# First slabs split and multiplied by single k, and the mixed activations moved behind the split weights, in a one-core decoder layer

## The chip, the cores and the metric

One NeuronCore of a Trainium2 chip runs the whole layer in one launch. The metric is the device time of that launch in microseconds (us); lower is better. Engines are named as the profile names them: PE is TensorE (matmuls), PEld its weight loads, DVE is VectorE, ACT is ScalarE, POOL is GpSimd, SP is SyncE, which here only issues DMAs.

## What is computed

One decoder layer on x of shape (1, 256, 2048), all in float32. Cut to what matters here:

```python
hn = rmsnorm(x, norm_mix_g)
p = hn @ w_in + b_in                        # 2048 x 7176: conv a and g, q, k, v, o, gates
u = silu(group_norm(causal_dwconv(p_a * sigmoid(p_g))))
hm = group_norm(mlstm(q, k, v, gates)) * sigmoid(p_o)
x = x + concat([u, hm]) @ w_out             # 2048 x 2048
hf = rmsnorm(x, norm_ffn_g)
up = hf @ w_up                              # 2048 x 11264
x = x + (silu(causal_dwconv(up[:, :5632])) * up[:, 5632:]) @ w_down   # 5632 x 2048
return rmsnorm(x, norm_final_g)
```

## The kernel before, in words

**Split matmuls.** Each float32 operand is written as a sum of a rounded part `hi` (type fp32r) and a remainder `lo`. A product is then three matmuls: hi by hi, hi by the other's low part, lo by hi. The weights come from memory in *slabs* of two k blocks of 128 rows by 512 columns (512 KB, 128 x 1024 in SBUF). `load(i)` (line 173) brings slab i into one of five `raw` buffers, by DMAs on SP's queue; `split` (190) and `split_part` (207) make `hi` by a cast on ACT (line 214; for one half of slab 0 by a copy on DVE, line 212) and `lo` by a subtraction on DVE or POOL (line 215). There are four buffers for each of `hi` and `lo`.

**The order of work** is written out by hand: each engine runs its instructions in the order in which the Python code issues them, and waits for others by semaphores. The loop over slabs (line 993) issues for slab i the load of slab i + 5, the splits of slabs ahead, the matmuls of slab i, and then what other work has been put on the list for this slab (`tasks`, `after`, `bg`). Splits run up to three slabs ahead.

**The start.** Slabs 0 to 7 are the first column group of the convolution's projection, `ws_group` (line 225): there the weights are the stationary operand (128 x 128 blocks, four column blocks `ct` for each k) and 256 columns of x, transposed, the moving one (tile `xp`, `xT["h"]` and `xT["l"]`). x itself is transposed beside them. `prep_x(c)` (line 924) does this for the two k blocks of slab c: four transposes on PE into a PSUM bank (line 928), the high part on ACT, scaled by the norm's gain (931), the low part on DVE (934). It is called from inside the matmuls of the slab before, by `mid_hook` (lines 235 and 1007). The DMAs on SP are, in order: the gain's rows, slab 0, x for slab 1, slab 1, x for slab 2, slab 2 and so on; x for slab 0 comes on ACT's queue. Slabs 0 and 1 are loaded in two DMAs of one k each (line 183), later slabs of this group in two DMAs of one column half each (185).

Ahead of slab 0, PE is given warm-up transposes of the identity matrix, `warm_pe` (949): six, then the transposes of the gain, five more, x's first block (k = 0 of slab 0), ten more. Slab 0 is split in halves, one for each k; x's second block and the second half come after the twelve matmuls of the first k, the transposes of x for slab 1 after six more.

The matmuls of a `ws` slab run k by k and, inside, ct by ct: three products on the same column block (lines 241 to 243) and then the next block.

**Where tiles lie.** Tile pools are laid one behind the other in SBUF: `cst`, then `slab` (five `raw`, four `hi`, four `lo`, 4,096 bytes per partition each), then `mid`. Within `mid`, tiles lie in the order in which they are first asked for: seven row tiles of 512 bytes, `bb` of 8,224 bytes, then `mixh` and `mixl` of 16,384 bytes each (lines 304 and 305), then the rest. When the feed-forward part begins, `mid` is closed and a pool `ffn` opens in its place (`open_ffn`), with `ah` and `al` first.

`mixh` and `mixl` are the split, concatenated outputs of the two head groups. They are the stationary operand of the output projection (w_out): `xs_slab` (line 277) with the slab's `hi` and `lo` as the moving operand of 512 columns, lines 286 to 288. The down projection runs the same lines with `ah` and `al`.

Of the kernel before, what the change touches and what calls it, by code (L numbers as in the profile page):

```python
# [9 lines left out]
F32 = mybir.dt.float32  # L10
F32R = mybir.dt.float32r
AF = mybir.ActivationFunctionType
# [3 lines left out]
P = 128  # L16
T = 256
NT = T // P
D = 2048
NK = D // P  # L20
# [14 lines left out]
SPLIT_BUFS = 4  # L35
AHEAD = 3
SIG = 4
WARM = (6, 5, 10)


@with_exitstack
def hybrid_layer_kernel(
# [7 lines left out]
    act, dve, pool, pe = nc.scalar, nc.vector, nc.gpsimd, nc.tensor  # L50
# [7 lines left out]
    mid = inner.enter_context(tc.tile_pool(name="mid", bufs=1))  # L58
# [3 lines left out]
    def mm_bank(name):  # L62
        return ps.tile([P, 512], F32, tag="mm", name=name, bufs=4)

    def cv_bank(k, name):
        return ps.tile([P, 512], F32, tag=f"cv{k}", name=name)

    def ax_bank(name):
        return ps.tile([P, 512], F32, tag="ax", name=name, bufs=2)
# [6 lines left out]

    def v2(t):
        return t.rearrange("p (a b) -> p a b", a=2)


    ident = cst.tile([P, P], F32, tag="ident", name="ident")
# [56 lines left out]
    g_mix = cst.tile([P, NK], F32, tag="cG", name="cG")  # L138
# [5 lines left out]
    def transpose_rows(*items):  # L144
        b = ax_bank("tr")
        o = 0
        for key, dst in items:
            r, n = rows[key]
            pe.transpose(b[:, o:o + n], r[:n, :], ident[:n, :n])
            o += n  # L150
        o = 0
        for key, dst in items:
            n = rows[key][1]
            act.copy(dst, b[:, o:o + n])
            o += n
# [6 lines left out]
    slabs = []  # L162
    tasks = defaultdict(list)
    bg = deque()
    cur = [0]

    def after(delay, fn, cost=0.0):
        tasks[cur[0] + delay].append((fn, cost))

    raw_t, hi_t, lo_t = {}, {}, {}  # L170
    mid_hook = []

    def load(i):
        if i >= len(slabs):
            return
        s = slabs[i]
        t = slab.tile([P, 2 * W], F32, tag="raw", name=f"raw{i}", bufs=RAW_BUFS)
        d = t[:, :s["nk"] * s["w"]]
        if len(s["src"].shape) == 4:
            d = d.rearrange("p (k s c) -> p k s c", k=s["nk"], s=2)  # L180
            for h in range(2):
                if i < 2:
                    nc.sync.dma_start(d[:, h], s["src"][:, h])
                else:
                    nc.sync.dma_start(d[:, :, h], s["src"][:, :, h])
        else:
            nc.sync.dma_start(d.rearrange("p (k c) -> p k c", k=s["nk"]), s["src"])
        raw_t[i] = t

    def split(i):  # L190
        if i >= len(slabs):
            return
        split_part(i, 0, 1, *split_tiles(i))

    def split_tiles(i):
        s = slabs[i]
        n = s["nk"] * s["w"]
        raw = raw_t.pop(i)
        hi = slab.tile([P, 2 * W], F32R, tag="hi", name=f"hi{i}", bufs=SPLIT_BUFS)
        lo = slab.tile([P, 2 * W], F32R, tag="lo", name=f"lo{i}", bufs=SPLIT_BUFS)  # L200
        s["eng"] = pool if s["pool"] and i >= 8 and i % 2 else dve
        hi_t[i] = hi[:, :n].rearrange("p (k c) -> p k c", k=s["nk"])
        lo_t[i] = lo[:, :n].rearrange("p (k c) -> p k c", k=s["nk"])
        s["lo"] = 0.0 if s["eng"] is pool else 1.1 * n + 30
        return raw, hi, lo

    def split_part(i, h, parts, raw, hi, lo):
        s = slabs[i]
        n = s["nk"] * s["w"]
        c = slice(h * n // parts, (h + 1) * n // parts)  # L210
        if h + 1 < parts:
            dve.tensor_copy(hi[:, c], raw[:, c])
        else:
            act.copy(hi[:, c], raw[:, c])  # L214
        s["eng"].tensor_sub(lo[:, c], raw[:, c], hi[:, c].bitcast(F32))  # L215

    def w_slab(wap, kt, nk, col, w, fn, on_pool):
        if col is None:
            src = wap(kt)
        else:  # L220
            src = wap[kt * P:(kt + nk) * P, col:col + w].rearrange("(k p) c -> p k c", p=P)
        slabs.append(dict(src=src, w=w, nk=nk, mm=fn, pool=on_pool))


    def ws_group(wap, col, mov, nk, done, on_pool):
        st = {}

        def mk(kt):
            def fn(hi, lo):
                if kt == 0:  # L230
                    st["b"] = [mm_bank("ws0"), mm_bank("ws1")]
                mh, ml = mov()
                for k in range(2):
                    for ct in range(4):
                        if mid_hook and mid_hook[0][0] == (k, ct):
                            mid_hook.pop(0)[1]()
                        o = v2(st["b"][ct // 2])[:, ct % 2, :]
                        cs = slice(ct * P, (ct + 1) * P)
                        first = kt + k == 0 and ct % 2 == 0
                        last = kt + k == nk - 1  # L240
                        pe.matmul(o, hi[:, k, cs], mh[:, kt + k, :], start=first, stop=False, skip_group_check=True)  # L241
                        pe.matmul(o, hi[:, k, cs], ml[:, kt + k, :], start=False, stop=False, skip_group_check=True)  # L242
                        pe.matmul(o, lo[:, k, cs], mh[:, kt + k, :], start=False, stop=last, skip_group_check=True)  # L243
                if kt + 2 == nk:
                    done(st["b"])
            return fn

        for kt in range(0, nk, 2):
            w_slab(wap, kt, 2, col, W, mk(kt), on_pool)
# [49 lines left out]
    xT = {}  # L299
# [1 line left out]
    def get_xT():  # L301
        return xT["h"], xT["l"]

    mixh = mid.tile([P, NK, T], F32R, tag="mixh", name="mixh")
    mixl = mid.tile([P, NK, T], F32R, tag="mixl", name="mixl")
    vt = mid.tile([P, NT, NH, HD + 2], F32, tag="vt", name="vt")
    og = mid.tile([P, NT, 3 * OW], F32, tag="og", name="og")
    wt = mid.tile([P, NH, 384], F32, tag="wt", name="wt")
# [612 lines left out]
        if c < RAW_BUFS:  # L921
            load(c)

    def prep_x(c, ks=(0, 1)):
        b = ax_bank("xT")
        for k in ks:
            for tt in range(NT):
                pe.transpose(b[:, k * T + tt * P:k * T + (tt + 1) * P], big[:, tt, (2 * c + k) * P:(2 * c + k + 1) * P], ident)
        for k in ks:
            kt = 2 * c + k  # L930
            act.activation(xT["h"][:, kt, :], v2(b)[:, k, :], AF.Copy, scale=g_mix[:, kt:kt + 1])
        for k in ks:
            kt = 2 * c + k
            dve.scalar_tensor_tensor(xT["l"][:, kt, :], v2(b)[:, k, :], g_mix[:, kt:kt + 1],
                                     xT["h"][:, kt, :].bitcast(F32), op0=ALU.mult, op1=ALU.subtract)

    def sq_x(hh):
# [11 lines left out]
    def warm_pe(n):  # L949
        b = cv_bank(0, "warm")  # L950
        for k in range(n):
            pe.transpose(b[:, 0:P], ident, ident)

    warm_pe(WARM[0])
    transpose_rows(("G", g_mix))
    warm_pe(WARM[1])
    prep_x(0, (0,))
    warm_pe(WARM[2])
    first = split_tiles(0)
    split_part(0, 0, 2, *first)  # L960
    tasks[7].append((sq_x(0), 0))
    tasks[8].append((sq_x(1), 0))
    tasks[9].append((rs_x, 200))
# [25 lines left out]

    n_p4 = p3_start + 32  # L990
    credit = 0.0
    split_next = [1]
    for i in range(len(slabs)):
        cur[0] = i
        load(i + RAW_BUFS)
        if i == 0:
            def second_k():
                prep_x(0, (1,))
                split_part(0, 1, 2, *first)
            mid_hook.append(((1, 0), second_k))  # L1000
        if i + 1 < NK // 2:
            def hook():
                prep_x(i + 1)
                while split_next[0] <= i + (1 if i < 3 else 2):
                    split(split_next[0])
                    split_next[0] += 1
            mid_hook.append(((1, 2) if i == 0 else (0, 0), hook))
        else:
            while split_next[0] <= i + AHEAD:
                split(split_next[0])  # L1010
                split_next[0] += 1
        slabs[i]["mm"](hi_t.pop(i), lo_t.pop(i))
        assert not mid_hook
        for d, h in at.get(i, []):
            after(d, lambda h=h: mlstm_scores(h), 600)
        if i == p3_start:
            load_x1()
        used = slabs[i]["lo"] + 100.0
        for fn, cost in tasks.pop(i, []):
            fn()  # L1020
            used += cost
        credit = min(credit + 2.54 * slabs[i]["nk"] * slabs[i]["w"] - used, 3000.0)
        first = True
        while bg and credit > 0:
            name = bg[0][0].__name__
            if name == "tail" and not first:
                break
            fn, cost = bg.popleft()
            fn()
            credit -= cost  # L1030
            first = False
            if name == "head" or name == "tail" and not bg:
                break
# [32 lines left out]
```

## Time and profile before

| | |
|---|---|
| median of 3 runs | 1137.03 us (1136.78 to 1137.9) |
| profiled execution, its own time | 1136.69 us |
| its span, first to last instruction | 1135.0 us |
| PE busy | 1122.2 us, 99% of the span |
| DVE, ACT, POOL busy | 746.3, 579.2, 131.1 us |
| DMA, mean over the span | 190 GB/s |

The span is what the profile sees; 1.69 us of the execution's own time lie around it. A busy engine is one with an instruction in it; matmuls overlap, so that the duration of one (its fill and its drain with it) is longer than the step from the start of one to the start of the next. A wait names the instruction that stood and the instruction whose end released it.

### The profile page before, as it was taken

The page shows a single profiled execution, that of the slowest core. Times are in us where ns is not written, and L with a number is a line of the kernel's source. Part 1 is how long each engine was busy: PE and PEld are TensorE (multiplying, and loading weights), DVE is VectorE, ACT ScalarE, POOL GpSimd, SP SyncE. Part 2 cuts the span into 40 slices and gives each one's busy share as a digit, 9 for nine tenths or more (in the row PEclk, how much of TensorE's full clock was granted, in tenths as well). Part 3 has the DMA queues.
Part 4 walks back from the last instruction along what each step waited for, and adds up shares of the span by engine and source line. Part 5 has one row for each costly group of instructions (what it writes and reads, how often), then busy time and mean ns, then how long its engine had stood idle before and what let it go on. Part 6 is the DMA issues. An engine that isn't in the chain of part 4 may idle for free.

```text
span 1135.0 us, 16970 instructions
## 1 busy us (share of the span) xinstructions
PE 1122.2 (99%) x6516; PEld 995.0 (88%) x6516; DVE 746.3 (66%) x1136; ACT 579.2 (51%) x822; POOL 131.1 (12%) x100
## 2 busy tenths in 40 slices
PE   8999999999999999999999999999999999999997
PEld 8999999998888888888888888888888888888886
DVE  5498999987656457667666676576676645454543
ACT  4744576754445455545545555455455534343443
POOL 0343554543200000000000000000000000000000
PEclk9999999999999999999999999999999999999999
DMA  8864665565555666666666666666666667656662
GB/s 266 254 184 127 178 220 170 179 193 176 193 197 174 184 184 184 192 197 187 185 199 190 185 189 193 192 186 188 194 194 184 191 195 230 195 191 194 193 193 90
DMA packets 122681, 215.40 MB, mean 190 GB/s; under 512 B 7440, under 2 KB 33256, under 8 KB 122088
## 3 DMA queue, kind: packets, MB, share of 16 engines
q1 hardware_dynamic: 121048, 209.92, 61.5%
q10 hardware_dynamic: 1552, 4.39, 1.0%
q8 instruction: 51, 0.84, 0.3%
q14 instruction: 30, 0.25, 0.1%
HBM read 212.19 MB, written 2.10 MB: 189 GB/s over the span
## 4 chain that ended last, share of the span: by engine, by line
PE 95%; DVE 3%; ACT 1%; issue 1%; POOL 0%; POOLq 0%; ACTq 0%
PE gate L267 14%; PE up L267 14%; PE xs L287 9%; PE xs L286 9%; PE xs L288 9%; PE up L268 7%; PE gate L268 7%; PE ws L243 5%; PE ws L241 5%; PE ws L242 5%; PE xs L841 2%; PE xs L840 2%; PE xs L842 2%; DVE conv L376 2%; DVE lo L215 1%
## 5 line engine op out<-in xcount | busy, mean ns | idle before, releaser
L215 DVE TENSOR_TENSOR lo<-raw,hi 128x1024 fp32r<-128x1024 f32 (+2 forms) x353 | 435.0, 1233 | 326.2 <-ACT hi L214 324.8
L214 ACT CAST hi<-raw 128x1024 fp32r<-128x1024 f32 (+2 forms) x400 | 411.8, 1033 | 452.5 <-PE xs L288 153.7
L267 PE MATMUL gate<-x1p,hi 128*128 128x512 f32 x704 | 245.0, 390 | 0.0
L267 PE MATMUL up<-x1p,hi 128*128 128x512 f32 x704 | 244.5, 390 | 0.0
L268 PE MATMUL up<-x1p,lo 128*128 128x256 f32 x704 | 198.5, 282 | 0.0
L268 PE MATMUL gate<-x1p,lo 128*128 128x256 f32 x704 | 198.5, 282 | 0.0
L267 PEld LDWEIGHTS up<-x1p,hi 128*128 128x128 f32 x704 | 132.2, 188 | 27.7
L267 PEld LDWEIGHTS gate<-x1p,hi 128*128 128x128 f32 x704 | 132.2, 188 | 27.6
L241 PE MATMUL ws<-xp,hi 128*128 128x256 f32 x512 | 145.1, 283 | 1.8 <-ACT hi L214 1.8
L243 PE MATMUL ws<-xp,lo 128*128 128x256 f32 x512 | 143.3, 280 | 1.5 <-DVE lo L215 1.5
L242 PE MATMUL ws<-xp,hi 128*128 128x256 f32 x512 | 143.0, 279 | 0.0
L268 PEld LDWEIGHTS gate<-x1p,lo 128*128 128x128 f32 x704 | 133.1, 189 | 0.0
L268 PEld LDWEIGHTS up<-x1p,lo 128*128 128x128 f32 x704 | 133.1, 189 | 0.0
L215 POOL TENSOR_TENSOR lo<-raw,hi 128x1024 fp32r<-128x1024 f32 (+1 forms) x48 | 110.5, 2304 | 152.4 <-ACT hi L214 114.4
L287 PE MATMUL xs<-lo,ah 128*128 128x512 f32 x264 | 102.7, 389 | 0.0
L286 PE MATMUL xs<-hi,ah 128*128 128x512 f32 x264 | 102.7, 389 | 0.0
L288 PE MATMUL xs<-hi,al 128*128 128x512 f32 x264 | 102.7, 389 | 0.0
L241 PEld LDWEIGHTS ws<-xp,hi 128*128 128x128 f32 x512 | 96.2, 188 | 3.0 <-ACT hi L214 2.3
L243 PEld LDWEIGHTS ws<-xp,lo 128*128 128x128 f32 x512 | 96.2, 188 | 2.5 <-DVE lo L215 2.3
L376 DVE SCALAR_TENSOR_TENSOR conv<-up,cB,conv 128x256 f32<-128x256 f32 x240 | 97.5, 477 | 0.0
L242 PEld LDWEIGHTS ws<-xp,hi 128*128 128x128 f32 x512 | 96.3, 188 | 0.0
L817 POOL TENSOR_TENSOR rf<-ms,halves 128x1 f32<-128x1 f32 x2 | 1.1, 551 | 711.7 <-DVE ms L811 711.7
(188 smaller groups left out, 1308.6 us busy)
## 6 DMA issues: line engine op xcount, KB each, us to landing
raw<-in_w_up_dram SPq DMA_DIRECT2D x176, 512.0 KB, 3.9
raw<-in_w_down_dram SPq DMA_DIRECT2D x88, 512.0 KB, 4.4
raw<-in_w_in_dram SPq DMA_DIRECT2D x48, 512.0 KB, 4.0
raw<-in_w_in_dram SPq DMA_DIRECT2D x64, 256.0 KB, 4.4
raw<-in_w_out_dram SPq DMA_DIRECT2D x32, 512.0 KB, 4.3
raw<-in_w_in_dram SPq DMA_DIRECT2D x24, 344.0 KB, 3.5
x<-in_x_dram ACTq DMA_DIRECT2D x2, 1024.0 KB, 8.0
xs<-in_x_dram SPq DMA_DIRECT2D x7, 256.0 KB, 5.3
```

What stands on the lines that cost most here:

```text
L214: act.copy(hi[:, c], raw[:, c])
L215: s["eng"].tensor_sub(lo[:, c], raw[:, c], hi[:, c].bitcast(F32))
L241: pe.matmul(o, hi[:, k, cs], mh[:, kt + k, :], start=first, stop=False, skip_group_check=True)
L242: pe.matmul(o, hi[:, k, cs], ml[:, kt + k, :], start=False, stop=False, skip_group_check=True)
L243: pe.matmul(o, lo[:, k, cs], mh[:, kt + k, :], start=False, stop=last, skip_group_check=True)
L267: pe.matmul(o, hi[:, k, cs], m2, start=first, stop=last, skip_group_check=True)
L268: pe.matmul(o[:, 0:T], lo[:, k, cs], mp[:, kt + k, 0, :], start=False, stop=last, skip_group_check=True)
L286: pe.matmul(o, sh[:, kt + k, ts_], hi[:, k, :w], start=first and k == 0, stop=False)
L287: pe.matmul(o, sh[:, kt + k, ts_], lo[:, k, :w], start=False, stop=False)
L288: pe.matmul(o, sl[:, kt + k, ts_], hi[:, k, :w], start=False, stop=last and k == 1)
L376: dve.scalar_tensor_tensor(a, up[c][:, t:t + T], cB[:, 8 * t + c:8 * t + c + 1], a, op0=ALU.mult, op1=ALU.add)
L840: pe.matmul(o, sh[:, kt, ts_], hi[:, k, c:c + cw], start=kt == first, stop=False, skip_group_check=True)
```

## The change

Four things are changed. (1) Slab 2 is loaded by single k as well (`BY_K = 3`). (2) Slabs 0, 1 and 2 are split in halves, one for each k, by hand-ordered calls: `split_part` is taken apart into `hi_part` and `lo_part`, `prep_x` into `x_turn`, `x_hi` and `x_lo`. The ten last warm-ups are gone, and x's two blocks for slab 0 are both transposed ahead of slab 0's matmuls. (3) In the first eight slabs the matmuls of one k run pass by pass: one product for all four column blocks, then the next product. The transposes of x for slab i + 1 stand between the two k of slabs 0 and 1, ahead of the first k from slab 2 on. (4) `mixh` and `mixl` are asked for first in the pool `mid`.

```diff
-WARM = (6, 5, 10)
+WARM = (6, 5)
+BY_K = 3
...
+    mixh = mid.tile([P, NK, T], F32R, tag="mixh", name="mixh")
+    mixl = mid.tile([P, NK, T], F32R, tag="mixl", name="mixl")
...
-                if i < 2:
+                if i < BY_K:
                     nc.sync.dma_start(d[:, h], s["src"][:, h])
...
     def split_part(i, h, parts, raw, hi, lo):
-        s = slabs[i]
-        n = s["nk"] * s["w"]
+        hi_part(i, h, parts, raw, hi, lo, act.copy)
+        lo_part(i, h, parts, raw, hi, lo)
+
+    def hi_part(i, h, parts, raw, hi, lo, copy):
+        n = slabs[i]["nk"] * slabs[i]["w"]
         c = slice(h * n // parts, (h + 1) * n // parts)
-        if h + 1 < parts:
-            dve.tensor_copy(hi[:, c], raw[:, c])
-        else:
-            act.copy(hi[:, c], raw[:, c])
-        s["eng"].tensor_sub(lo[:, c], raw[:, c], hi[:, c].bitcast(F32))
+        copy(hi[:, c], raw[:, c])
+
+    def lo_part(i, h, parts, raw, hi, lo):
+        n = slabs[i]["nk"] * slabs[i]["w"]
+        c = slice(h * n // parts, (h + 1) * n // parts)
+        slabs[i]["eng"].tensor_sub(lo[:, c], raw[:, c], hi[:, c].bitcast(F32))
...
                 for k in range(2):
-                    for ct in range(4):
-                        if mid_hook and mid_hook[0][0] == (k, ct):
-                            mid_hook.pop(0)[1]()
+                    if mid_hook and mid_hook[0][0] == k:
+                        mid_hook.pop(0)[1]()
+                    hh, hl, lh = (hi, mh), (hi, ml), (lo, mh)
+                    i = cur[0]
+                    if i >= NK // 2:
+                        steps = [(ct, a) for ct in range(4) for a in (hh, hl, lh)]
+                    else:
+                        steps = [(ct, a) for a in ((hh, lh, hl) if i + k == 0 else (hh, hl, lh)) for ct in range(4)]
+                    for ct, (w, m) in steps:
                         o = v2(st["b"][ct // 2])[:, ct % 2, :]
-                        cs = slice(ct * P, (ct + 1) * P)
-                        first = kt + k == 0 and ct % 2 == 0
-                        last = kt + k == nk - 1
-                        pe.matmul(o, hi[:, k, cs], mh[:, kt + k, :], start=first, stop=False, skip_group_check=True)
-                        pe.matmul(o, hi[:, k, cs], ml[:, kt + k, :], start=False, stop=False, skip_group_check=True)
-                        pe.matmul(o, lo[:, k, cs], mh[:, kt + k, :], start=False, stop=last, skip_group_check=True)
+                        first = kt + k == 0 and ct % 2 == 0 and w is hi and m is mh
+                        pe.matmul(o, w[:, k, ct * P:(ct + 1) * P], m[:, kt + k, :], start=first,
+                                  stop=kt + k == nk - 1 and w is lo, skip_group_check=True)
...
-    mixh = mid.tile([P, NK, T], F32R, tag="mixh", name="mixh")
-    mixl = mid.tile([P, NK, T], F32R, tag="mixl", name="mixl")
...
-    def prep_x(c, ks=(0, 1)):
-        b = ax_bank("xT")
+    x_bank = {}
+
+    def x_turn(c, ks=(0, 1)):
+        b = x_bank[c] = ax_bank("xT")
         for k in ks:
             for tt in range(NT):
                 pe.transpose(b[:, k * T + tt * P:k * T + (tt + 1) * P], big[:, tt, (2 * c + k) * P:(2 * c + k + 1) * P], ident)
+
+    def x_hi(c, ks=(0, 1)):
         for k in ks:
             kt = 2 * c + k
-            act.activation(xT["h"][:, kt, :], v2(b)[:, k, :], AF.Copy, scale=g_mix[:, kt:kt + 1])
+            act.activation(xT["h"][:, kt, :], v2(x_bank[c])[:, k, :], AF.Copy, scale=g_mix[:, kt:kt + 1])
+
+    def x_lo(c, ks=(0, 1)):
         for k in ks:
             kt = 2 * c + k
-            dve.scalar_tensor_tensor(xT["l"][:, kt, :], v2(b)[:, k, :], g_mix[:, kt:kt + 1],
+            dve.scalar_tensor_tensor(xT["l"][:, kt, :], v2(x_bank[c])[:, k, :], g_mix[:, kt:kt + 1],
                                      xT["h"][:, kt, :].bitcast(F32), op0=ALU.mult, op1=ALU.subtract)
...
     warm_pe(WARM[0])
     transpose_rows(("G", g_mix))
+    x_turn(0, (0,))
+    x_hi(0, (0,))
     warm_pe(WARM[1])
-    prep_x(0, (0,))
-    warm_pe(WARM[2])
-    first = split_tiles(0)
-    split_part(0, 0, 2, *first)
+    p0 = split_tiles(0)
+    hi_part(0, 0, 2, *p0, dve.tensor_copy)
+    lo_part(0, 0, 2, *p0)
+    x_lo(0, (0,))
+    x_turn(0, (1,))
+    x_hi(0, (1,))
+    hi_part(0, 1, 2, *p0, act.copy)
+    x_lo(0, (1,))
+    lo_part(0, 1, 2, *p0)
+
+    def prep_1():
+        p1 = split_tiles(1)
+        x_turn(1)
+        x_hi(1)
+        hi_part(1, 0, 2, *p1, dve.tensor_copy)
+        x_lo(1, (0,))
+        lo_part(1, 0, 2, *p1)
+        hi_part(1, 1, 2, *p1, act.copy)
+        x_lo(1, (1,))
+        lo_part(1, 1, 2, *p1)
+
+    def prep_2():
+        p2 = split_tiles(2)
+        hi_part(2, 0, 2, *p2, act.copy)
+        x_turn(2)
+        x_hi(2)
+        lo_part(2, 0, 2, *p2)
+        hi_part(2, 1, 2, *p2, act.copy)
+        x_lo(2)
+        lo_part(2, 1, 2, *p2)
+
+    def prep(i):
+        def f():
+            x_turn(i)
+            x_hi(i)
+            x_lo(i)
+            while split_next[0] <= i + (i > 4):
+                split(split_next[0])
+                split_next[0] += 1
+        return f
...
-    split_next = [1]
+    split_next = [BY_K]
...
-        if i == 0:
-            def second_k():
-                prep_x(0, (1,))
-                split_part(0, 1, 2, *first)
-            mid_hook.append(((1, 0), second_k))
         if i + 1 < NK // 2:
-            def hook():
-                prep_x(i + 1)
-                while split_next[0] <= i + (1 if i < 3 else 2):
-                    split(split_next[0])
-                    split_next[0] += 1
-            mid_hook.append(((1, 2) if i == 0 else (0, 0), hook))
+            mid_hook.append((1, (prep_1, prep_2)[i]) if i < 2 else (0, prep(i + 1)))
```

## Rows read from the trace of the kernel before

**Rows 1.** Page, part 1: busy time of each engine, share, instructions

```profile
PE 1122.2 (99%) x6516; PEld 995.0 (88%) x6516; DVE 746.3 (66%) x1136; ACT 579.2 (51%) x822; POOL 131.1 (12%) x100
```

**Rows 2.** Waits of PE, whole span: total us, times, longest us

```profile
PE ws L241 <- ACT hi L214: 1.8, 2, 1.1
PE ws L243 <- DVE lo L215: 1.5, 3, 0.7
```

**Rows 3.** Timeline of PE, 0 to 24 us: start, length of the run, instructions

```profile
1.42 1.54 PE L952 MATMUL warm<-ident 128*128 128x128 f32 x6 [1.42 <-POOL ident masks.py:199]
...
4.66 2.20 PE L952 MATMUL warm<-ident 128*128 128x128 f32 x10
6.62 0.36 PE L241 MATMUL ws<-xp,hi 128*128 128x256 f32 x1
...
8.35 0.38 PE L928 MATMUL xT<-ident,xs 128*128 128x128 f32 x2
...
13.56 0.39 PE L241 MATMUL ws<-xp,hi 128*128 128x256 f32 x1 [0.71 <-ACT hi L214]
...
14.82 0.38 PE L243 MATMUL ws<-xp,lo 128*128 128x256 f32 x1 [0.75 <-DVE lo L215]
...
17.52 0.60 PE L928 MATMUL xT<-ident,xs 128*128 128x128 f32 x4
...
20.76 0.60 PE L928 MATMUL xT<-ident,xs 128*128 128x128 f32 x4
```

**Rows 4.** Tile xs, 0 to 30 us: PE's transposes of x, ns min/median/max

```profile
L928 PE MATMUL xT<-ident,xs x28: 270/272/421, 4.2 to 27.6; 128*128 128x128 f32 x28
```

**Rows 5.** Windows: busy us of PE, PEld, DVE, ACT, POOL, granted clock, DMA share, GB/s

```profile
0.00:7.00 7.00, 5.58 (x26) 5.07 (x26) 1.67 (x6) 2.06 (x4) 1.26 (x16) 1.00 0.74 210
8.50:18.00 9.50, 6.74 (x52) 5.86 (x50) 5.19 (x8) 4.43 (x8) 0.00 (x0) 1.00 1.10 352
```

**Rows 6.** Tiles mixh and hi, whole span: one matmul form each, ns min/median/max

```profile
L286 PE MATMUL xs<-hi,mixh x128: 392/396/579, 302.3 to 397.2; 128*128 128x512 f32 x128
...
L286 PE MATMUL xs<-hi,ah x264: 389/389/392, 887.4 to 1066.3; 128*128 128x512 f32 x132
```

**Rows 7.** Timeline of PE, 350 to 353 and 950 to 953 us

```profile
350.02 0.40 PE L286 MATMUL xs<-hi,mixh 128*128 128x512 f32 x1
...
352.82 0.40 PE L286 MATMUL xs<-hi,mixh 128*128 128x512 f32 x1
...
950.20 0.39 PE L287 MATMUL xs<-lo,ah 128*128 128x512 f32 x1
...
952.92 0.39 PE L287 MATMUL xs<-lo,ah 128*128 128x512 f32 x1
```

**Rows 8.** Timeline of DVE, 5 to 7 us

```profile
5.48 0.48 DVE L934 SCALAR_TENSOR_TENSOR xp<-xT,cG,xp 128x256 fp32r<-128x256 f32 x1 [4.40 <-ACT xp L931]
5.88 0.42 DVE L212 CAST hi<-raw 128x512 fp32r<-128x512 f32 x1
6.33 0.69 DVE L215 TENSOR_TENSOR lo<-raw,hi 128x512 fp32r<-128x512 f32 x1
```

**Rows 9.** Tile raw, 3.0 to 3.7 us: slab 1's two loads and their landing

```profile
L183 SPq DMA_DIRECT2D raw<-in_w_in_dram x2: 469/470/470, 2.7 to 3.2; - x2
...
DMA to landing us min/median/max: 4.7/4.8/4.9
```

**Rows 10.** Timeline of ACT, 9 to 10 us

```profile
9.14 0.61 ACT L214 CAST hi<-raw 128x512 fp32r<-128x512 f32 x1
```

**Rows 11.** Waits of PE, 60 to 300 us: total us, times, longest us

```profile
PE ws L243 <- DVE lo L215: 0.5, 1, 0.5
PE xs L287 <- DVE lo L215: 0.4, 1, 0.4
```

**Rows 12.** Windows, columns as in rows 5: output projection, down projection

```profile
310.00:390.00 80.00, 80.00 (x358) 64.80 (x357) 45.58 (x65) 37.52 (x54) 3.79 (x6) 1.00 0.60 192
900.00:1000.00 100.00, 100.00 (x443) 82.84 (x442) 47.64 (x41) 40.07 (x41) 0.00 (x0) 1.00 0.65 205
```

## The prediction

> **What bounds the kernel now.** I read the page's busy times first: TensorE (PE) is busy for 1122.2 of 1135.0 us [rows 1], so time can come only from PE's own rate or from the few places where PE stands. The waits say where those are: two on ScalarE's `hi` (1.8 us) and three on VectorE's `lo` (1.5 us) [rows 2]. All but one come before 15 us, so I went to PE's timeline of the start. The reader should see three stretches there [rows 3]. Up to 6.62 us PE runs only transposes, ten warm-up ones from 4.66 on. From 6.62 to 17.52 it works by fits and starts. From 17.52 on each slab takes 3.24 us (to 20.76), four transposes of x and 24 matmuls, with no gap.
>
> Steady prices: four transposes take 4 x 0.11 us, where 0.11 is a pair's 0.38 less one transpose's 0.27 [rows 3, 4]; a 256-wide matmul then takes (3.24 - 0.44) / 24 = 0.117 us. From 6.62 to 17.52 PE does 48 matmuls and ten transposes, 5.6 + 1.1 = 6.7 us of work in 10.9 us. So **4.2 us** are lost there.
>
> The rate is not constant at the start. The windows grant a clock of 1.00 from 0 us on [rows 5], the 2.4 GHz level; yet the slowest transpose takes 421 ns against a median of 272 [rows 4], and the ten warm-ups, 4.66 to 6.62, are 0.20 us apart against 0.11 later. That is the 1.2 GHz level. The first twelve matmuls, 6.62 to 8.35, take 1.73 us where 1.40 is the steady price, so the rate has risen by about 6.5 us, some 5.1 us after the first transpose at 1.42, while PE ran without a long pause.
>
> The second place is PE's rate where it never stands. In the output projection a 512-wide matmul takes 396 ns, in the down projection, by the same code line, 389 [rows 6]; by starts, 350.02 to 352.82 is 12 matmuls of 0.2333 us and 950.20 to 952.92 is 12 of 0.2267 [rows 7].
>
> **The change, part by part.**
>
> *First matmul.* Ten warm-ups (4.66 to 6.62) go, and k = 0's two transposes go ahead of the other five, so x's first parts are ready sooner and wait for the weights. k = 1's pair moves ahead of slab 0; at the low rate it costs 2 x 0.21, and PE is free at 4.66 + 0.42 = 5.1 us. VectorE now starts with the cast of raw half 0, which the trace shows at 5.88 [rows 8], behind other work, so the landing is at latest there. My estimate is from the queue: slab 1's first half, issued at 2.73, landed 4.7 us later, at 7.4 [rows 9]; it is three 256 KB transfers behind slab 0's first, 0.79 MB at 352 GB/s [rows 5], 2.2 us. So the half lands at 5.2, the cast (0.42) ends at 5.6, the first matmul starts at about 5.65 instead of 6.62. Bounds: 5.1 (PE's own queue) and 6.35 (landing at 5.88).
>
> *The clock.* With the rise at 6.5 as before, the first four matmuls run at half rate: 0.4 us lost.
>
> *Fits and starts.* The order by passes (four `hi`-`hi`, four with `lo`, four with x's low part) lets PE begin on a cast alone; VectorE's subtraction (0.69) runs beside four matmuls. Do the feeders keep up? VectorE has up to the end of slab 1: two casts of 0.42, four subtractions of 0.69, four x parts at 0.40 (their step from 5.48 to 5.88) [rows 8], 5.2 us, from 5.2 to 10.4. By the sum below PE wants the last of these at about 12.0. Slab 2's second half, three transfers behind slab 1's (issued at 3.2, landed 4.9 us later, at 8.1 [rows 9]), lands at 10.3; its casts are on ScalarE (0.61 each [rows 10]), its `lo` is ready by about 13, wanted at 15. So PE should not stand after its first matmul. Up to the transposes of x for slab 3, at 17.52 before, it does 48 matmuls and eight transposes, 6.5 us: 5.65 + 0.4 + 6.5 = 12.5. **Gain 5.0 us** (4.6 from the late landing, 5.2 from the early one).
>
> *Costs at nothing.* Slab 2's load still is two DMAs of 256 KB, cut by k instead of by column half; SP issues as many as before, and loads that follow are released earlier because `lo` ends earlier. Extra split instructions are VectorE's and ScalarE's, covered by the slack just counted; without it, 0.4 to 0.7 us each. Slab 5's split comes one slab later, 3.24 us ahead of its first matmul; it needs one cast and one subtraction of a whole slab, at most twice the halves in [rows 8, 10], 1.2 and 1.4 us, behind the x parts. The pass order gives PE no more instructions. Whether alternating weights change the rate no row shows: 192 matmuls by the 3% by which [rows 7] differ, at most 0.65 us either way; I take 0. From slab 8 on the order is the old one. What carries the lead to the end: behind the first slabs PE has two waits in all, of 0.5 and 0.4 us [rows 11], so all that follows moves up with it.
>
> *Placement.* `mixh` and `mixl`, the weights PE loads in the output projection, now open the pool `mid`, directly behind the slab pool. Before, seven row tiles of 512 bytes and `bb` of 8,224 lie ahead, 11,808 bytes, not a multiple of 64. The pool `ffn` opens where `mid` began, with `ah` first; so `mixh` now gets exactly the address of `ah`, against the same `hi` and `lo`. If the address makes the difference of [rows 6, 7], the projection's 32 slabs x 12 = 384 matmuls get 0.0067 us shorter each: **2.5 us**. The lower bound is 0; a loss as large, -2.5, no row excludes. I take 2.5, as one line with one shape and the same moving tiles differs by nothing else that I find except the load: VectorE is busy for 45.6 of 80 us there and 47.6 of 100 in the other [rows 12], yet the matmuls of each stretch keep their step.
>
> The Trainium skill ("TensorE: Matmul & The Clock Gate", Part 2, step on LDWEIGHTS) says the stationary and the moving operand have read ports of their own, so that loading weights takes nothing from the running matmul. By that rule the place of `mixh` is worth nothing and the sum ends 2.5 us higher; the 396 against 389 ns leave room for doubt of it.
>
> Sum: 1136.69 (profiled execution; span 1135.0, 1.69 around it) - 5.0 - 2.5 = 1129.2; the median of the runs, 1137.03, stands 0.34 above that execution, so **1129.5**.
>
> **Rivals.**
> 1. *The place is worth nothing*, because the longer step comes from the load beside the matmuls. For it: VectorE's higher share there [rows 12]. Against: the even step. Time: 1137.03 - 5.0 = 1132.0.
> 2. *The clock rises later.* Without the ten warm-ups PE pauses from 5.1 to 5.65; if the rise then comes as late after this pause as it came after the first transpose, it comes at 10.75. PE then runs 4.25 us at half rate, 2.1 us lost: 1131.6. Against: in the old start the waits of up to 1.1 us, soon after the rise, left the rate high [rows 2, 3]. The Trainium skill (same page, Part 4) says that transposes don't count as PE activity in the usual way; by that rule only matmuls raise the clock and this rival would hold. The trace disagrees: only transposes ran ahead of the rise at 6.5 [rows 3].
> 3. *Slower: the clock stays low.* If the thinner start leaves PE at 1.2 GHz, each 0.117 us matmul costs 0.117 more. The point at which the 7.5 us are eaten is a rise 15 us later than before, at 21.5; over the whole first group (192 matmuls, 28 transposes) the loss is 25 us and the time 1155. Against: by the sum PE works almost without a pause from 5.65 us on, while the old start, with its waits, kept the rate.
> 4. *The start gains nothing much and the place neither*: the landing or VectorE is the true pace of the first slabs. For it: the DMA engines are busy throughout there, at 352 GB/s [rows 5]. Against: from 17.52 on the same feeders and queues held 3.24 us a slab without a wait [rows 3]. Time: about 1136.
>
> **How the numbers follow.** Forecast 0.60 (1128.5 to 1130.5); rival 1 0.19; rival 2 0.12; rival 4 0.06; rival 3 0.03. The range takes the forecast, rivals 1 and 2, with the bounds 4.6 to 5.2 and the 0.65 of the pass order: 1127.7 to 1133.3; a placement that costs 2.5 us (1134.5) is left out with rivals 3 and 4. 0.2%, what a measurement of this kernel can tell, is 2.3 us: the forecast and rivals 1 and 2 are faster by more (0.91), rival 4 is no change (0.06), rival 3 slower (0.03).
>
> **What would show it.** Right: the first matmul at 5.1 to 6.3; no waits of PE on `hi` or `lo` ahead of slab 3; the transposes that were at 17.52 near 12.5; later slabs some 5 us earlier throughout; 512-wide matmuls on `mixh` at 389 ns. Wrong: these still at 396 (rival 1); matmuls 0.2 us apart after 7 us (rival 2); PE waiting for `lo` or a DMA in slabs 1 and 2 (rival 4); or the lead shrinking between 30 and 60 us, where the load of `bb` and POOL's subtractions are.

## The result, and the profile after

The changed kernel takes 1130.97 us (median of 6 runs, 1130.23 to 1131.26) against 1137.03 (6 runs): the ratio is 0.9945, with a 95% interval of 0.9933 to 0.9958. The profiled execution took 1131.08 us, its span is 1129.3 us against 1135.0, so 5.7 us are to be found in the two traces.

PE's waits of the whole span first (total us, times, longest):

```profile
PE warm L968 <- POOL ident masks.py:199: 1.4, 1, 1.4
PE xT L940 <- DMA xs<-in_x_dram: 0.5, 1, 0.5
PE ws L254 <- DVE lo L224: 0.5, 1, 0.5
PE xs L299 <- DVE lo L224: 0.4, 1, 0.4
```

Against [rows 2], the waits on ACT's `hi` and all but one of those on DVE's `lo` are gone; that one and the wait of L299 are the two of [rows 11], far behind the start. New is a wait of 0.5 us of x's transposes for a DMA. PE's timeline of the start shows where it lies (start, length of the run, instructions):

```profile
3.65 1.27 PE L968 MATMUL warm<-ident 128*128 128x128 f32 x5
5.46 0.66 PE L940 MATMUL xT<-ident,xs 128*128 128x128 f32 x2 [0.54 <-DMA xs<-in_x_dram]
5.77 1.20 PE L254 MATMUL ws<-xp,hi 128*128 128x256 f32 x4
6.77 1.05 PE L254 MATMUL ws<-xp,lo 128*128 128x256 f32 x4
7.62 1.05 PE L254 MATMUL ws<-xp,hi 128*128 128x256 f32 x4
8.48 0.93 PE L940 MATMUL xT<-ident,xs 128*128 128x128 f32 x4
9.17 1.19 PE L254 MATMUL ws<-xp,hi 128*128 128x256 f32 x8
10.19 0.63 PE L254 MATMUL ws<-xp,lo 128*128 128x256 f32 x4
...
12.06 0.60 PE L940 MATMUL xT<-ident,xs 128*128 128x128 f32 x4
...
13.91 0.60 PE L940 MATMUL xT<-ident,xs 128*128 128x128 f32 x4
...
17.16 0.60 PE L940 MATMUL xT<-ident,xs 128*128 128x128 f32 x4
```

Three things are to be seen. From 5.77 us on PE never stands in this stretch. The first twelve matmuls take 5.77 to 8.48, 0.23 us each, so the whole of them ran at half rate; only from 9.17 on are they 0.12 us apart. And slab 3's transposes, at 17.52 before [rows 3], are at 13.91: a lead of 3.6 us.

The moment at which the rate rises can also be read from the trace's record of the granted clock. It begins with the entry of the full clock (2.4 GHz), at 9.2 us in this profile and at 6.6 in that of the kernel before. Ahead of this entry there is none, so the granted clock of 1.00 that [rows 5] show from 0 us on says nothing of that stretch; its steps, twice as long as later, say 1.2 GHz.

The lead is kept: the output projection begins 3.51 us earlier. It then ends 5.67 us earlier, which the first matmul of the projection and the first behind it show, before

```profile
302.25 0.48 PE L286 MATMUL xs<-hi,mixh 128*128 128x512 f32 x1
...
397.93 0.40 PE L267 MATMUL gate<-x1p,hi 128*128 128x512 f32 x1
```

and after:

```profile
298.74 0.48 PE L298 MATMUL xs<-hi,mixh 128*128 128x512 f32 x1
...
392.26 0.40 PE L279 MATMUL gate<-x1p,hi 128*128 128x512 f32 x1
```

So the projection takes 93.52 us instead of 95.68, 2.16 less. The forms answer to [rows 6]: the matmuls on `mixh` now take what those on `ah` take.

```profile
L298 PE MATMUL xs<-hi,mixh x128: 389/389/578, 298.7 to 391.6; 128*128 128x512 f32 x128
```

3.51 + 2.16 = 5.67 us: the two places hold the whole difference of the spans, and the gate, up and down projections are as long as before (the first two 489.47 and 489.49 us).

### The profile page after: what moved, and what is told of

Read it like the earlier page. It is cut to its first block, busy times and chain, and to the rows that moved or that the text cites. A ratio compares the mean times of both kernels' runs of the same rounds, so it can differ in the third digit from the quotient of the medians.

```text
span 1129.3 us, 16955 instructions
## 1 busy us (share of the span) xinstructions
PE 1118.7 (99%) x6506; PEld 994.4 (88%) x6506; DVE 746.0 (66%) x1139; ACT 578.9 (51%) x823; POOL 131.6 (12%) x100
## 4 chain that ended last, share of the span: by engine, by line
PE 95%; DVE 3%; ACT 1%; issue 1%; DMA 0%; ACTq 0%; POOLq 0%; POOL 0%
PE ws L254 16%; PE gate L279 14%; PE up L279 14%; PE xs L298 9%; PE xs L299 9%; PE xs L300 9%; PE up L280 8%; PE gate L280 8%; PE xs L852 2%; PE xs L850 2%; PE xs L851 2%; DVE conv L386 2%; DVE lo L224 1%; DMA xs<-in_x_dram 0%; PE xT L940 0%
## 5 line engine op out<-in xcount | busy, mean ns | idle before, releaser
L254 PE MATMUL ws<-xp,hi 128*128 128x256 f32 x1024 | 178.5, 282 | 0.0
L254 PEld LDWEIGHTS ws<-xp,hi 128*128 128x128 f32 x1024 | 153.4, 189 | 0.8 <-issue 0.3
L254 PE MATMUL ws<-xp,lo 128*128 128x256 f32 x512 | 135.5, 280 | 0.5 <-DVE lo L224 0.5
L299 PE MATMUL xs<-lo,ah 128*128 128x512 f32 x264 | 102.7, 389 | 0.0
L254 PEld LDWEIGHTS ws<-xp,lo 128*128 128x128 f32 x512 | 93.2, 189 | 0.9 <-DVE lo L224 0.7
L300 PEld LDWEIGHTS xs<-hi,al 128*128 128x128 f32 x264 | 49.6, 188 | 10.4
L298 PEld LDWEIGHTS xs<-hi,ah 128*128 128x128 f32 x264 | 49.6, 188 | 10.4
```

The lines of the kernel that those rows point to most:

```text
L254: pe.matmul(o, w[:, k, ct * P:(ct + 1) * P], m[:, kt + k, :], start=first, stop=kt + k == nk - 1 and w is lo, skip_group_check=True)
L298: pe.matmul(o, sh[:, kt + k, ts_], hi[:, k, :w], start=first and k == 0, stop=False)
L299: pe.matmul(o, sh[:, kt + k, ts_], lo[:, k, :w], start=False, stop=False)
L300: pe.matmul(o, sl[:, kt + k, ts_], hi[:, k, :w], start=False, stop=last and k == 1)
```

## The experiments

Times of one session stand beside the kernel before of that session: 1136.81, 1136.79 and 1137.06 us. Runs are called by the first part of their names, e1 to e11; each left one profile.

### The two parts alone

```diff
+    mixh = mid.tile([P, NK, T], F32R, tag="mixh", name="mixh")   # e1_place: before,
+    mixl = mid.tile([P, NK, T], F32R, tag="mixl", name="mixl")   # asked for first
     ident = cst.tile([P, P], F32, tag="ident", name="ident")
```

> The kernel before, with mixh and mixl asked for first in the pool mid and nothing else changed. Theory: the place alone shortens the output projection by 2.2 us (95.68 us before, 93.52 us in the changed kernel), 512-wide matmuls on mixh at 389 ns instead of 396, ratio to before about 0.998, and the start as before, with slab 3's transposes of x at 17.5 us. Rival (the matmuls are shorter because the work around them shifted with the start): 396 ns and no change of time.

Measured: 1134.65 us (11 runs), ratio 0.9981 (0.9972 to 0.999), 389 ns, a projection of 93.53 us, and the old start. The place does it alone, by the forecast 2.2 us.

The other part (e2) is the changed kernel with these two lines back in their old place.

> The changed kernel with mixh and mixl back behind the row tiles and bb. Theory: it keeps the start's gain alone, 3.5 us (the output projection begins at 298.74 instead of 302.25 us), the 512-wide matmuls on mixh go back to 396 ns, about 1133.2 to 1133.5 us, ratio 0.997. Rival: the two parts work only together, 1131.0 or 1137.0.

Measured: 1132.7 us (5 runs, 1132.28 to 1133.82), ratio 0.9965 (0.9952 to 0.9978), the projection 95.67 us long and at 396 ns again. In medians the parts add up: 2.2 + 4.1 us, against 6.1 for both.

The profiled execution of this run showed something I had not looked for. Its start, by the same code, is much better than that of the changed kernel:

```profile
5.29 0.41 PE L940 MATMUL xT<-ident,xs 128*128 128x128 f32 x2 [0.33 <-DMA xs<-in_x_dram]
5.46 0.71 PE L252 MATMUL ws<-xp,hi 128*128 128x256 f32 x4
...
7.06 0.60 PE L940 MATMUL xT<-ident,xs 128*128 128x128 f32 x4
...
12.15 0.60 PE L940 MATMUL xT<-ident,xs 128*128 128x128 f32 x4
```

Here the rate rose at 5.0 us, just inside PE's pause ahead of x's second block (4.96 to 5.29): the first four matmuls take 0.55 us. Slab 3 is 5.4 us ahead of [rows 3], a little more than I forecast. Yet the projection begins at 299.37, only 2.9 us ahead, and this execution, at 1133.82 us, was the slowest of the five. PE's waits and ACT's timeline tell where the lead went:

```profile
PE ws L252 <- POOL lo L222: 0.9, 1, 0.9
PE rsb L340 <- ACT dg L335: 0.6, 1, 0.6
```

```profile
38.05 1.05 ACT L217 CAST hi<-raw 128x1024 fp32r<-128x1024 f32 x1 [2.52 <-DMA raw<-in_w_in_dram]
```

Slab 11's weights land at 38 us, as in the changed kernel (its cast at 37.28), whenever PE wants them: SP's queue has seven small row loads and `bb`'s 1 MB ahead of them. The cast, POOL's subtraction (39.17 to 41.55) and the square sums that stand on ACT behind the cast come late, and PE waits. Taken instruction by instruction against the kernel before, the lead is 5.4 us up to the first wait, 4.2 behind it and 3.3 behind the second; the last 0.4 us go between 130 and 200 us and were not traced. A later run (448 bytes, below), 4.4 us ahead at slab 3, had the same two waits, 1.0 and 0.6 us, and in e3 (next) the lead went from 4.2 to 3.7 us at the second of them, there 0.2 us long. So there is a **second bound**, a cap of some 3.3 to 3.7 us on the lead at about 45 us. It is no cap on the lead at the projection: e3's grew again behind it, to 4.0 us there, for a reason not traced.

### What sets the rise of PE's rate

```diff
-WARM = (6, 5)
+WARM = (6, 8)      # e3_warm8
```

> The changed kernel with eight warm-up transposes instead of five in the second stretch: three more of 0.21 us, which fill PE's pause from 4.92 to 5.46 us. Theory: the pause, in which PE waits for x's second block, put off the rise of PE's rate; with it filled the rate rises at about 6.5 us again, as in the kernel before, and the time falls by 1.2 us to about 1129.8. Rival: the pause has no part in it (the removed warm-up transposes ahead of 6.5 us are not made up for by matmuls that come in their place, or the moment differs from run to run), the rate rises at about 9.1 us and the time stays at 1131.0.

Measured: 1130.95 us (5 runs, 1129.53 to 1132.2), ratio 0.9947 (0.9934 to 0.996). The wait for x's DMA is gone and PE runs without a pause; yet in

```profile
5.68 1.20 PE L254 MATMUL ws<-xp,hi 128*128 128x256 f32 x4
6.68 1.05 PE L254 MATMUL ws<-xp,lo 128*128 128x256 f32 x4
7.53 0.85 PE L254 MATMUL ws<-xp,hi 128*128 128x256 f32 x4
8.22 0.60 PE L940 MATMUL xT<-ident,xs 128*128 128x128 f32 x4
```

the rate rises at 8.0 us, not 6.5. My theory, that the pause put it off, falls as stated: the rise was earlier than 9.2, but not where it had been, and the median did not move. In e2 the rate even rose inside the pause.

```diff
     x_turn(0, (1,))
+    warm_pe(10)        # e10_warm10
     x_hi(0, (1,))
```

> The changed kernel with ten warm-up transposes put back right ahead of slab 0's first matmul. So far PE's rate rose at 6.4 to 7.1 us in each profile with the ten warm-ups there, and at 5.6, 7.9, 8.9, 9.1 and 9.3 us without. Theory (an unbroken run of transposes sets the rise; matmuls at half rate in their place put it off): the rise comes by 7.1 us again, the first matmul at about 7.6, the transposes of x for slab 3 at about 14.1 us, time 1131.0 to 1131.4, and the executions lie as close together as those of the kernel before (0.7 us; 1.0 to 2.7 us without the ten). Rival (the moment differs from execution to execution, whatever PE does): rises later than 7.6 us occur here too, the matmuls after the ten begin at half rate, executions spread over more than 1 us, median 1131.5 or more.

Measured: 1131.42 us (5 runs, 1130.88 to 1132.49), ratio 0.9953 (0.994 to 0.9965).

```profile
5.87 1.68 PE L968 MATMUL warm<-ident 128*128 128x128 f32 x10
7.30 0.71 PE L254 MATMUL ws<-xp,hi 128*128 128x256 f32 x4
...
13.88 0.60 PE L940 MATMUL xT<-ident,xs 128*128 128x128 f32 x4
```

The ten transposes take 1.43 us from start to start of what follows: four at 0.21 and the rest at 0.11; the rate rose at 6.7 us. Slab 3 is reached at 13.88, the same as without them (13.91): what the early rise gives is what the ten cost. That part came as the theory has it. The closeness of the executions did not: they spread over 1.6 us. The moments of the rise, by the record of the granted clock in each profile; the steps change from 0.21 to 0.12 or 0.11 us at the same places:

| PE's work ahead of the first matmul | rise in each profile, us |
|---|---|
| with ten warm-ups right ahead | 5.7 (e4), 6.2 (e6_pad480), 6.6 (before), 6.7 (e10), 7.3 (e1), 7.5 (e6_pad96) |
| without | 5.0 (e2), 7.6 (e11_off448), 8.0 (e3), 8.9 (e8), 9.2 (changed), 9.3 (e11_off256), 11.0 (e5), 12.0 (e9) |

The moments in e10's expectation were read less closely: its 5.6 is 5.0, and its bounds of 6.4 to 7.1 leave out four of the profiles with the ten warm-ups. Without the ten, the rise came later than in any profile with them in seven of eight; but in six profiles whose work up to there is the same but for addresses (e2, e5, e8, both of e11 and the changed kernel) it lies between 5.0 and 11.0 us, a wider spread than lies between the two rows of the table. What sets the moment stays **open**.

### The order by passes

```diff
-                    if i >= NK // 2:
+                    if i >= 0:          # e9_by_block: three products per block everywhere
```

> The changed kernel with the matmuls of the first eight slabs back in the old order, three products on one column block and then the next; loads, splits and transposes stay as changed. Theory: the passes give VectorE's subtractions the time of four matmuls; without them PE waits for x's low part at its second matmul (ready at about 6.5 us) and for lo in slab 1 (ready at 11.4 us, wanted at about 10.9): 1.0 to 1.5 us given back, 1132.0 to 1132.5, with waits of PE on VectorE ahead of 15 us. Rival (the order of the feeders does it all): no new waits, 1131.0.

Measured: 1132.42 us (5 runs, 1130.68 to 1132.79), ratio 0.9957 (0.9943 to 0.997), 1.45 us more than the changed kernel's median. The intervals overlap and one run of the five was at 1130.68, so the size is not sharp. The profile has the one expected wait in slab 0,

```profile
5.71 0.56 PE L254 MATMUL ws<-xp,hi 128*128 128x256 f32 x1
6.57 0.58 PE L254 MATMUL ws<-xp,hi 128*128 128x256 f32 x1 [0.30 <-DVE xp L950]
...
11.86 0.49 PE L254 MATMUL ws<-xp,hi 128*128 128x256 f32 x2
```

where the second matmul starts 0.86 us behind the first, but none in slab 1, and the rate rises only at 12.0 us. Slab 3 is reached at 15.56. I read it so: the passes save some 0.6 us in slab 0; the rest of the 1.65 us to 13.91 is the late rise of this execution.

### The loads that cap the lead

```diff
-    tasks[1].append((load_vectors, 0))
+    tasks[6].append((load_vectors, 0))    # e8_late
+    tasks[16].append((load_bb, 0))        # taken out of load_late, slab 5
```

> The changed kernel with the seven small loads of rows_A moved from slab 1's list to slab 6's, and bb's load from slab 5's to slab 16's (they are needed from slab 10 and from slab 40 on). Theory: SP, held at these small loads from 15 to 21 us, and bb's 1 MB ahead of slab 11 cap the lead that PE can keep at some 3.5 us: in the run of the start alone a lead of 5.4 us at slab 3 shrank to 2.85 us at the output projection, with waits on POOL's lo and on the norm. Without them the DMA has no gap at 20 to 22 us, PE no wait at 40 to 50 us, and the time falls by 0.5 to 1.5 us, to 1129.5 to 1130.5; the executions in which PE's rate rises early gain, those in which it rises late don't. Rival (the rise of the rate alone sets the lead): 1131.0 as now.

Measured: 1130.86 us (5 runs, 1129.88 to 1131.32), ratio 0.9944 (0.9931 to 0.9958): no change from 1130.97. The gap in the DMA is filled; the window from 20 to 22 us (columns as in [rows 5]), first the changed kernel, then this one:

```profile
20.00:22.00 2.00, 2.00 (x19) 2.00 (x19) 0.91 (x2) 0.96 (x3) 0.00 (x0) 1.00 0.06 18
```

```profile
20.00:22.00 2.00, 2.00 (x20) 2.00 (x19) 0.92 (x2) 1.16 (x3) 0.00 (x0) 1.00 1.10 346
```

Slab 11 is cast at 36.02 without a wait. But the rate rose at 8.9 us in the profiled execution, and its lead, 3.8 us at slab 3 and still 3.8 behind the place of the two waits, was hardly more than the cap. So the cap is shown by the waits of three profiles, and this one shows that the moved loads had held slab 11 back (its cast began at 37.28 to 38.40 in the profiles with the loads in their place). That taking the cap away is worth anything in the median is not shown.

### What in the place counts

```diff
+    mid.tile([P, 8], F32, tag="pad", name="pad")   # e4_pad32; 24 and 120 columns: e6_pad96, e6_pad480
     mixh = mid.tile([P, NK, T], F32R, tag="mixh", name="mixh")
```

> The kernel before, with 32 unused bytes per partition ahead of mixh: mixh and mixl stay behind the row tiles and bb, 11,840 bytes behind the split weights instead of 11,808, a multiple of 64 now. Theory: what counts is how mixh lies to hi and lo modulo 64 bytes, so the matmuls on mixh take 389 ns and the output projection is 2.2 us shorter, as with the tiles directly behind. Rival: they must lie next to the split weights (or at the address of ah); then 396 ns and no change.

> The kernel before with 96 unused bytes ahead of mixh: 11,904 bytes behind the split weights, a multiple of 128, not of 256. With 32 bytes (a multiple of 64) the matmuls on mixh had 394 ns, against 396 and 389. Theory: the place counts modulo 128 bytes: 389 ns and the output projection 2.2 us shorter. Rivals: modulo 256 or more, then 394 to 396 here and 389 with 480 bytes; or nearness alone, then 394 to 396 in both.

> The kernel before with 480 unused bytes ahead of mixh: 12,288 bytes behind the split weights, a multiple of 4,096. Theory (the place counts modulo some power of two up to 4,096): 389 ns on mixh and the output projection in 93.5 us instead of 95.7. Rival (tiles must lie directly behind): 394 to 396 ns and 95.7 us.

Measured: 1137.02 us (ratio 1.0002, 0.9993 to 1.0012) with 32 bytes, 1136.98 with 96 and 1134.34 with 480 (one run each). The form's rows in this order:

```profile
L286 PE MATMUL xs<-hi,mixh x128: 393/394/578, 302.3 to 397.4; 128*128 128x512 f32 x128
```

```profile
L286 PE MATMUL xs<-hi,mixh x128: 390/393/589, 302.5 to 397.5; 128*128 128x512 f32 x128
```

```profile
L286 PE MATMUL xs<-hi,mixh x128: 389/389/587, 302.0 to 394.9; 128*128 128x512 f32 x128
```

The projection takes 95.77, 95.67 and 93.57 us. Nearness is not it: with 480 bytes `mixh` lies 12,288 bytes away, behind the row tiles and `bb`, and has all of the gain. Multiples of 64 and 128 bytes are not enough; 4,096 is. The runs below narrow this down to 256.

If the distance counts, `xp`, an operand of every matmul of the input, gate and up projections, could gain far more:

```diff
     xT["p"] = cst.tile([P, NK, 2, T], F32R, tag="xp", name="xp")
+    cst.tile([P, 136], F32, tag="pad1", name="pad1")   # e5_align; 120 and 200 columns: e11_off448, e11_off256
```

> The changed kernel with 544 unused bytes behind xp, so that the slab buffers and all behind them move up by 544 and hi and lo lie a multiple of 1,024 bytes behind xp (57,344 instead of 56,800); mixh, ah and hi keep their distances. Theory (what counts is how the two operands of a matmul lie to each other): the matmuls with xp as an operand shorten too. 512-wide ones with xp as the weights go from 396 to 389 ns, the 256-wide ones of the first groups from 280 to 276, a step of 0.1167 to 0.1133, the 512-wide ones of the gate and up projections from 0.230 to 0.2267; over 1536, 288, 192 and 2816 matmuls up to 5 + 1.3 + 1.3 + 9 us, time down to 1115 to 1125. Rival (only the place of the output projection's tiles counts, or the absolute address): no change, or the matmuls on mixh and ah go back to 396.

> The changed kernel with 480 unused bytes behind xp: hi and lo lie at 448 modulo 512 bytes behind xp, instead of 480 (the changed kernel) and 0 (544 unused bytes, where gate and up took 498.75 us instead of 489.48). No theory holds for both signs so far; this is to see the shape. If the step falls on with the distance from 0, gate and up end below 489.5 and the whole below 1131; if 480 is a low point of its own, they end above it.

> The changed kernel with 800 unused bytes behind xp: hi and lo lie at 256 modulo 512 bytes behind xp. As in the run with 448: if the step falls with the distance from 0, gate and up take less than 489.5 us; if what counts is only whether the distance is a multiple of 512, they take about 489.5; if 480 is a low point of its own, more.

Measured: 1142.91 us with 544 bytes (ratio 1.0052, 1.0039 to 1.0064), 1141.16 with 480 and 1142.59 with 800 (one run each). All three are slower than both kernels. Gate and up take 498.75, 498.73 and 498.75 us against 489.49; with 544 bytes that is 9.3 of the 12.4 us between the spans, and another 3.0 lie ahead of the output projection. The 512-wide form of the gate projection, in the changed kernel and with 544 bytes:

```profile
L279 PE MATMUL gate<-x1p,hi x704: 390/390/480, 392.3 to 859.2; 128*128 128x512 f32 x176
```

```profile
L279 PE MATMUL gate<-x1p,hi x704: 389/398/478, 395.3 to 871.1; 128*128 128x512 f32 x176
```

Not all of it went that way. The 512-wide matmuls that have `xp` as their weights and the slab as the moving operand (255 to 295 us) went from 395 to 389 ns, as I had expected. The rows of one of their three lines, in the changed kernel, then with 544 and with 800 bytes:

```profile
L299 PE MATMUL xs<-lo,xp x48: 392/395/398, 255.0 to 294.4; 128*128 128x512 f32 x48
```

```profile
L299 PE MATMUL xs<-lo,xp x51: 387/389/396, 254.7 to 295.0; 128*128 128x512 f32 x51
```

```profile
L299 PE MATMUL xs<-lo,xp x49: 387/389/397, 255.3 to 294.2; 128*128 128x512 f32 x49
```

With 480 bytes the three lines have 394 to 398 ns. The matmuls on `mixh` and `ah` stayed at 389 in all three runs, though both of their operands had moved by 544, 480 or 800 bytes: the distance counts, not the address. So one rule fits every 512-wide matmul here that has the activations as its weights: a distance that is a multiple of 256 bytes gives 389 ns in the median (0 modulo 512 with e1, e6_pad480 and e5, 256 with e11_off256), and the others tried, 32, 64, 128, 448 and 480 modulo 512, give 392 to 398. Where the slab is the weights, in gate and up, 0 and 256 are alike too, but on the slow side: the old odd distance, 480, is better than the three others. Why stays open.

## Why the prediction held, and which of its steps did not

1130.97 us lies inside the range, 1127.7 to 1133.3, but outside the band of the forecast itself, 1128.5 to 1130.5, and nearer to rival 2's 1131.6 than to 1129.5. Of the signs, the first matmul, the waits and the 389 ns came as written; slab 3's transposes did not (13.91 against 12.5), and rival 2's sign, matmuls 0.2 us apart after 7 us, did appear.

**The first matmul**: 5.65 forecast, 5.77 measured, but for another reason. The first half of the weights was cast at 5.00 us, so its landing was as worked out or a little better (5.2).

```profile
5.00 0.43 DVE L219 CAST hi<-raw 128x512 fp32r<-128x512 f32 x1 [3.92 <-DMA raw<-in_w_in_dram]
```

What came last was x's second block, a DMA on ACT's queue that my sum left out: its transposes stand ahead of slab 0 on PE and waited 0.54 us.

**The clock**: this term failed. I took the rise at 6.5 us as before, and a loss of 0.4 us. From 5.77 the work of 6.48 us up to slab 3's transposes would end at 12.25; it ended at 13.91, so the loss is 1.66 us. Rival 2 had the later rise, and 2.1 us for it, though by a reason, the pause, that e2 and e3 don't bear out; I gave it 0.12, because the old start's waits had left the rate high once it had risen. That was the wrong evidence: it speaks of keeping the rate, not of reaching it. The one moment of the rise that I had came from one execution, and the profiles since put it between 5.0 and 12.0 us. On the rule of the Trainium skill ("TensorE: Matmul & The Clock Gate", Part 4) that transposes don't count as PE activity in the usual way, the runs agree with the trace of before and not with the page: the rate rose at 6.7 us in e10 and at 5.0 in e2, ahead of the first matmuls at 7.30 and 5.46, with nothing but transposes before it. Whether these float32 transposes run in the mode that the page speaks of, no run shows.

**Fits and starts**: right. PE has no wait on `hi` or `lo` ahead of slab 3, DVE and ACT kept up, and the 4.2 us are gone. With 1.66 us of clock where I had 0.4, and a start 0.12 us later, 5.0 became 3.6.

**What carries the lead to the end**: right in the profiled execution, by luck. I argued that everything behind moves up with PE because PE had no waits there. SP's queue does not move up: its seven small loads go out one by one from 15.1 to 21.0 us, and `bb` stands ahead of slab 11. With the 5.0 us that I forecast, some of it would have been given back, as e2's 5.4 us became 2.9; the last of my signs had named this place, 30 to 60 us. Two errors of mine partly cancelled: with the lead held down by the late rise, the cap did not bite.

**Placement**: right in kind, a little large in size: 2.16 us instead of 2.5. The step after is what I took, 12 matmuls in 2.72 us (380.22 to 382.94). Over all 374 steps from one of these matmuls to the next, the two traces differ by 2.13 us, 5.7 ns a step; my 6.7 ns came from two stretches of 12 matmuls [rows 7]. Rival 1 is excluded by e1: nothing but the address changed. The rule of the Trainium skill (same page, Part 2, the step on LDWEIGHTS), that weight loads have a read port of their own and take nothing from the running matmul, would have made the place worth nothing. The runs differ from it: with both streams unchanged but for an address, a 512-wide matmul took 389, 393, 394 or 396 ns. Whether it is the weight load or the moving operand that the address holds up, no run shows.

**Rivals 3 and 4** did not occur in any profile: the latest rise, 12.0 us, is far from the 21.5 at which it would have cost the gain.

## What to carry to other kernels

When a kernel is bound by one engine, look at its rate as well as its gaps: two groups of the same line and shape with different durations are a lead, and an address may be all that differs. A lead won at the start reaches the end only if the loads behind it move up too; follow the DMA queue as far as the lead is to go. A time that hangs on the moment at which the clock rises should be taken from several profiles, not from one.

## What the runs showed of the hardware that was not expected

The distance between a matmul's two operands in SBUF changes its step by some 3%, in either direction and by the same amount in every profile; a multiple of 256 bytes is good where the activations are the weights, and bad in gate and up, where the slab is: the output projection took 93.52 to 93.62 us in ten profiles with the good place and 95.67 to 95.77 in four with another, and gate and up 489.47 to 489.49 or 498.73 to 498.75. Padding by a few hundred bytes between two tiles cost up to 12 us of 1131.

The rise of PE's rate at the start is not fixed in time by the program: 5.0, 8.9 and 9.2 us in three profiles whose work up to there is the same (e2, e8 and the changed kernel).
